# One-hots by pairs of tokens, six landing buffers and whole weight units in a two-layer s5, NSA and PEER kernel

## The chip, the cores and the metric

The kernel runs on 1 core of one Trainium2 chip. The metric is the device time of one execution in microseconds (us). A core has TensorE (PE: matmuls, with its weight loads listed apart as PEld), VectorE (DVE), ScalarE (ACT), GpSimd (POOL), and SyncE (SP), whose DMA queue brings the weights here.

## The reference

Two layers on 256 tokens of width 1024. Layer 0 mixes the tokens with an s5 state-space mixer, layer 1 with NSA attention; after each mixer comes a PEER layer: each token picks 16 of 16384 one-vector experts for each of 8 heads. Most of the time goes into PEER:

```python
def peer(h, w_q, sub_keys, u_tab, v_tab):
    qk = (h @ w_q).reshape(b, s, H, 2, PEER_HALF)
    sc = jnp.einsum('bshcd,hckd->bshck', qk, sub_keys)
    s1, i1 = lax.top_k(sc[..., 0, :], K)
    s2, i2 = lax.top_k(sc[..., 1, :], K)
    cand = (s1[..., :, None] + s2[..., None, :]).reshape(b, s, H, K * K)
    cidx = (i1[..., :, None] * PEER_NKEYS + i2[..., None, :]).reshape(b, s, H, K * K)
    top_s, top_pos = lax.top_k(cand, K)
    experts = jnp.take_along_axis(cidx, top_pos, axis=-1)
    gates = jax.nn.softmax(top_s, axis=-1)
...
        act = jax.nn.gelu(jnp.einsum('cd,ced->ce', hc, u)) * gc    # u = u_tab[experts]
        return jnp.einsum('ce,ced->cd', act, v)                    # v = v_tab[experts]
```

Around both stands `x = x + g * f(modulate(rmsnorm(x), sh, sc))`, with g, sh and sc from one product of the condition vector with `ada_w`; at the end comes an rmsnorm.

## The kernel before

Everything is held transposed (features on the 128 partitions, tokens along the row). The kernel doesn't gather experts: in each PEER layer it multiplies the hidden state with all 16384 rows of `peer_u`, in 128 units of 128x1024 32-bit values (512 KB), applies gelu, multiplies by a dense matrix of gates that is zero wherever no expert was picked, and multiplies the result, B (128 partitions x 128 x 256 tokens), with all 128 units of `peer_v`.

*Weight units.* `load_unit` (L126) brings a unit by SP's queue into one of five `raw` buffers (RAW, L25). `split_w` (L144) makes from it a rounded part w_hi (ACT, L139) and a rest w_lo (DVE, L181), each as two halves of 128x512, in rings of four buffers. `mm3` (L184 to 190) does three matmuls of 256 columns for each 128 rows: w_hi with h_hi, w_hi with h_lo, w_lo with h_hi; a unit has 8 x 3 of them. `chunk_T` does one unit; a `Pair` does two units in turns (at the input projection, glu, the first head of each routing, the first keys and the output projection).

*PEER's stages.* `route_steps` scores the keys and picks the top 16 with DVE's MAX, MAX_INDEX and MATCH_REPLACE (L863 to 867); `decode` turns positions into indices and gates (L919 to 943, with POOL's products at L931) and puts them into `slotT` by a transposition. `G` builds the dense gates for four tokens at a time, in 64 groups a layer: one-hots `oi` and `oj` of the picked row and column (DVE, L760 and 761), `oh` and `ol`, the column's one-hot times the two 16-bit parts of the gate (DVE L762, POOL L763), then eight 16-bit matmuls that sum the outer products into a PSUM bank (L767, L768), and a multiplication into B by DVE (L771) where gelu has been done already, or a copy by ACT (L774) where it hasn't (then L738 multiplies later). `VS` (L790 ff.) does the second product: per unit 12 matmuls of 512 columns into four banks (L797).

*Order.* Each engine takes its instructions in the program's order. That order is set by the tile scheduler by priorities and its own estimate of each operation; splits of weights have a higher priority (PRIO). `weave` puts U (the first product's units) beside the routing and then beside G, by the rough costs that each step yields. In `decode` DVE's order, and in VS DVE's and SP's order, is as written.

## Time and profile before

| | |
|---|---|
| time of 3 runs | median 2117.07 us (2114.87 to 2120.47) |
| profiled execution, its own time | 2114.4 us |
| span in its trace | 2112.6 us, 39866 instructions |
| mean granted clock of TensorE | 0.983 |
| PE busy | 2052.1 us, 97% |
| DVE busy | 1667.1 us, 79% |
| ACT busy | 1163.2 us, 55% |
| POOL busy | 271.0 us, 13% |
| DMA queue of the weights | 371.42 MB, 55.1% of 16 engines' span |

Busy time is the union of an engine's instructions; matmuls overlap in the pipeline, so that the duration of one says less than the distance of two starts. The span is that of the trace; the execution's own time lies around it.

### The profile page before, as it was taken

What the parts mean: (1) busy time and instruction counts of PE and PEld (TensorE: products, weight loads), DVE (VectorE), ACT (ScalarE), POOL (GpSimd) and SP (SyncE); (2) the same over time, 40 slices, a digit from 0 to 9 for tenths busy, and PEclk for the clock granted to TensorE, in tenths of its full rate; (3) what the DMA queues carried; (4) which work ended last, traced back from release to release, by engine and by line L of the source; (5) the groups of instructions that cost most, each with busy time, mean ns of one, the idle gap of its engine ahead of it and who ended that gap; (6) DMA issues with size and microseconds to landing.
All of it is one profiled execution on the core that took longest, in us unless ns stands there. A gap on an engine that the chain in (4) does not pass through costs nothing.

```text
span 2112.6 us, 39866 instructions
## 1 busy us (share of the span) xinstructions
PE 2052.1 (97%) x14344; PEld 1855.0 (88%) x14344; DVE 1667.1 (79%) x3826; ACT 1163.2 (55%) x2392; POOL 271.0 (13%) x277
## 2 busy tenths in 40 slices
PE   6899999999999999999999999999999999999998
PEld 3688999899999988888898689998999998888887
DVE  8696899889898777777766769999988975665655
ACT  4775555555445555555545655555554455555554
POOL 4230002223331000000010000023332300000000
PEclk8899999999999999999999999999999999999999
DMA  7445455544445888878863035554444456666663
GB/s 264 170 161 160 161 179 170 152 145 134 140 137 179 259 274 269 272 270 270 269 215 102 20 121 170 170 170 150 138 140 135 138 172 185 194 197 191 197 191 109
DMA packets 102695, 377.23 MB, mean 179 GB/s; under 512 B 11488, under 2 KB 11872, under 8 KB 101472
## 3 DMA queue, kind: packets, MB, share of 16 engines
q1 hardware_dynamic: 101520, 371.42, 55.1%
q0 software_dynamic: 544, 2.61, 0.4%
q8 instruction: 112, 1.84, 0.4%
q14 instruction: 87, 0.71, 0.1%
q10 hardware_dynamic: 432, 0.65, 0.1%
HBM read 373.07 MB, written 1.05 MB: 177 GB/s over the span
## 4 chain that ended last, share of the span: by engine, by line
PE 90%; DVE 6%; ACT 2%; issue 1%; DMA 0%; POOL 0%; DVEq 0%; ACTq 0%; POOLq 0%
PE bank L797 33%; PE bank L190 15%; PE bank L189 14%; PE bank L188 14%; PE bank L767 3%; PE bank L768 3%; DVE w_lo L181 2%; PE bank L1189 1%; PE bank L874 1%; PE bank L1152 1%; PE bank L1067 1%; PE bank L613 1%; PE bank L1150 1%; PE bank L1177 1%; PE bank L584 1%
## 5 line engine op out<-in xcount | busy, mean ns | idle before, releaser
L139 ACT ACTIVATE w_hi<-raw 128x512 fp32r<-128x512 f32 x1194 | 747.4, 629 | 641.4 <-PE bank L189 336.6
L181 DVE TENSOR_TENSOR w_lo<-raw,w_hi 128x512 fp32r<-128x512 f32 x1194 | 826.3, 715 | 120.4 <-ACT w_hi L139 117.8
L188 PE MATMUL bank<-h_hi,w_hi 128*128 128x256 f32 x2504 | 719.2, 290 | 10.6 <-ACT w_hi L139 7.2
L190 PE MATMUL bank<-h_hi,w_lo 128*128 128x256 f32 x2504 | 711.9, 287 | 13.2 <-DVE w_lo L181 13.0
L189 PE MATMUL bank<-h_lo,w_hi 128*128 128x256 f32 x2504 | 711.9, 285 | 1.0 <-DVE h_lo L304 1.0
L188 PEld LDWEIGHTS bank<-h_hi,w_hi 128*128 128x128 f32 x2504 | 483.5, 194 | 19.0 <-ACT w_hi L139 9.9
L190 PEld LDWEIGHTS bank<-h_hi,w_lo 128*128 128x128 f32 x2504 | 481.1, 193 | 18.0 <-DVE w_lo L181 17.6
L189 PEld LDWEIGHTS bank<-h_lo,w_hi 128*128 128x128 f32 x2504 | 484.2, 193 | 3.3 <-DVE h_lo L304 2.1
L797 PE MATMUL bank<-w_lo,a_hi 128*128 128x512 f32 x1024 | 398.9, 390 | 0.5 <-DVE w_lo L181 0.5
L797 PE MATMUL bank<-w_hi,a_lo 128*128 128x512 f32 x1024 | 398.5, 389 | 0.0
L797 PE MATMUL bank<-w_hi,a_hi 128*128 128x512 f32 x1024 | 281.3, 389 | 0.0
L181 DVE TENSOR_TENSOR a_lo<-B,a_hi 128x256 fp32r<-128x256 f32 x256 | 108.8, 425 | 193.6 <-ACT a_hi L139 193.6
L797 PEld LDWEIGHTS bank<-w_lo,a_hi 128*128 128x128 f32 x1024 | 192.2, 188 | 40.3 <-DVE w_lo L181 1.2
L797 PEld LDWEIGHTS bank<-w_hi,a_lo 128*128 128x128 f32 x1024 | 192.3, 188 | 40.0
L797 PEld LDWEIGHTS bank<-w_hi,a_hi 128*128 128x128 f32 x1024 | 191.4, 188 | 38.6
L763 POOL TENSOR_TENSOR ol<-oj,slotT 128x512 f16<-128x512 f16 x128 | 155.3, 1221 | 335.9 <-PE bank L768 323.8
L774 ACT ACTIVATE B<-bank 128x296 f32<-128x296 f32 (+31 forms) x128 | 67.6, 528 | 148.4 <-DVE B L771 148.4
L768 PE MATMUL bank<-ol,oi 128*128 128x128 f16 x512 | 126.6, 297 | 0.0
L767 PE MATMUL bank<-oh,oi 128*128 128x128 f16 x512 | 125.7, 295 | 0.0
L139 ACT ACTIVATE a_hi<-B 128x256 fp32r<-128x256 f32 x256 | 106.8, 418 | 27.3 <-PE bank L797 14.6
L771 DVE SCALAR_TENSOR_TENSOR B<-bank,B 128x216 f32<-128x216 f32 (+31 forms) x128 | 114.4, 893 | 1.1 <-ACT B L734 0.8
L762 DVE TENSOR_TENSOR oh<-oj,slotT 128x512 f16<-128x512 f16 x128 | 58.6, 459 | 42.7 <-PE bank L767 42.3
(267 smaller groups left out, 2067.8 us busy)
## 6 DMA issues: line engine op xcount, KB each, us to landing
raw<-peer_u SPq DMA_DIRECT2D x256, 512.0 KB, 3.6
raw<-peer_v SPq DMA_DIRECT2D x256, 512.0 KB, 4.3
raw<-ada_t SPq DMA_DIRECT2D x56, 512.0 KB, 4.3
raw<-ada_w SPq DMA_DIRECT2D x40, 512.0 KB, 5.3
raw<-w_q SPq DMA_DIRECT2D x32, 512.0 KB, 3.5
raw<-w_glu SPq DMA_DIRECT2D x16, 512.0 KB, 4.3
raw<-w_in SPq DMA_DIRECT2D x8, 512.0 KB, 4.8
w<-w_cmp SPq DMA_DIRECT2D x4, 1024.0 KB, 9.7
```

Of the source, the lines that this page charges most:

```text
L139: nc.scalar.activation(hi, raw, AF.Copy)
L181: K.nc.vector.tensor_tensor(lo, raw, hi.bitcast(F32), op=OP.subtract)
L188: nc.tensor.matmul(out, wh, xh, start=start, stop=False)
L189: nc.tensor.matmul(out, wh, xl, start=False, stop=False)
L190: nc.tensor.matmul(out, wl, xh, start=False, stop=stop)
L762: V.tensor_tensor(oh, oj, sl[2], op=OP.mult)
L763: nc.gpsimd.tensor_tensor(ol, oj, sl[3], op=OP.mult)
L767: nc.tensor.matmul(pv[:, t], oi[:, :, t], oh[:, :, t], start=True, stop=False)
L768: nc.tensor.matmul(pv[:, t], oi[:, :, t], ol[:, :, t], start=False, stop=True)
L771: V.scalar_tensor_tensor(Bv[:, ts, :jd], pv[:, :, :jd], 1.0 / GS, Bv[:, ts, :jd], op0=OP.mult, op1=OP.mult)
L774: nc.scalar.activation(Bv[:, ts, jd:], pv[:, :, jd:], AF.Copy, scale=1.0 / GS)
L797: nc.tensor.matmul(acc[t][dh], a[al][:, ts], w[wl], start=(j == 0 and al + wl == 0), stop=(j == NJ - 1 and al == 1))
```

## The change

The constant `iota4` (each number four times) becomes `iota2` (twice). G makes all one-hots of a group in one comparison of 1024 values (`oij`: two pairs of tokens, row or column, 128 places, two tokens) and both products with the gate in one multiplication of 1024 (`ohl`), both on DVE; POOL has no part in it. `slotT` gets the matching order, written by two ACT operations where one stood. The matmuls read their operands at a step of two 16-bit values where it was four, and write their result at a step of four 32-bit values where it was without gaps; the multiplication into B then runs over B and the bank in the order in which both lie. A unit's w_hi and w_lo are made by one operation of 128x1024 each, in rings of two buffers. RAW becomes 6, `ge` has one buffer, and `cact` lies in layer 0's pool.

```diff
@@ -22,7 +22,7 @@
 DEPTH = 2
 EPS = 1e-6
 PRIO = 200
-RAW = 5
+RAW = 6
 TWO_PI = 2.0 * math.pi
 C1 = 6.28125
 C2 = TWO_PI - C1
@@ -58,15 +58,10 @@
     nc.scalar.dma_start(K.cst, aps["consts"])
     K.ident = K.cst[:, 0:P]
     K.iota = K.cst[:, P:2 * P]
-    K.iota4 = K.const.tile([P, 4 * P], F16, name="iota4")
-    nc.vector.tensor_copy(K.iota4.rearrange("p (j t) -> p j t", t=4), K.iota[:, :, None].to_broadcast([P, P, 4]))
+    K.iota2 = K.const.tile([P, P, 2], F16, name="iota2")
+    nc.vector.tensor_copy(K.iota2, K.iota[:, :, None].to_broadcast([P, P, 2]))
     K.ones = K.const.tile([P, P], F32, name="ones")
     nc.vector.memset(K.ones, 1.0)
-
-
-    K.cact = K.const.tile([P, KC, 32], F32, name="cact")
-    nc.gpsimd.memset(K.cact, 0.0)
-    silu(K, K.cact[:, :, 0], small(K, "c"))
 
     K.mod = [K.const.tile([P, 48], F32, name=f"mod{i}") for i in range(DEPTH)]
 
@@ -77,6 +72,11 @@
             break
         with tc.tile_pool(name=f"x{layer}", bufs=1, reuse_waits="tile") as xp:
             K.xp = xp
+            if not layer:
+
+                K.cact = xp.tile([P, KC, 32], F32, name="cact")
+                nc.gpsimd.memset(K.cact, 0.0)
+                silu(K, K.cact[:, :, 0], small(K, "c"))
             if layer:
                 peer_end(K, 0, acc)
             mixer(K)
@@ -144,15 +144,14 @@
 def split_w(K, raw):
 
     with K.tc.high_priority(offset=PRIO):
-        return [split(K, raw[:, i * 512:(i + 1) * 512], [P, 512], "w", bufs=4) for i in range(2)]
+        return split(K, raw, [P, 1024], "w", bufs=2)
 
 
 def chunk_T(K, w, x, out):
 
     for k in range(KC):
-        hi, lo = w[k // 4]
-        cs = slice((k % 4) * P, (k % 4 + 1) * P)
-        mm3(K, out, (hi[:, cs], lo[:, cs]), (x[0][:, k], x[1][:, k]), k == 0, k == KC - 1)
+        cs = slice(k * P, (k + 1) * P)
+        mm3(K, out, (w[0][:, cs], w[1][:, cs]), (x[0][:, k], x[1][:, k]), k == 0, k == KC - 1)
 
 
 class Pair:
@@ -164,10 +163,9 @@
         self.ps = [bank(K)[:, :S] for _ in srcs]
 
     def add(self, k):
-        cs = slice((k % 4) * P, (k % 4 + 1) * P)
+        cs = slice(k * P, (k + 1) * P)
         for w, ps in zip(self.ws, self.ps):
-            hi, lo = w[k // 4]
-            mm3(self.K, ps, (hi[:, cs], lo[:, cs]), (self.x[0][:, k], self.x[1][:, k]), k == 0, k == KC - 1)
+            mm3(self.K, ps, (w[0][:, cs], w[1][:, cs]), (self.x[0][:, k], self.x[1][:, k]), k == 0, k == KC - 1)
 
 
 def pair_T(K, srcs, x):
@@ -716,7 +714,7 @@
             tc.tile_pool(name=f"pw{layer}", bufs=2, reuse_waits="tile") as wp, ExitStack() as es:
 
         B = pp.tile([P, NJ, S], F32, name="B")
-        slotT = pp.tile([P, 4, S], F16, name="slotT")
+        slotT = pp.tile([P, 2, S // 2, 2, 2], F16, name="slotT")
         done = [0]
         ugelu = [0]
         u_src, v_src = K.aps["peer_u"], K.aps["peer_v"]
@@ -733,7 +731,7 @@
                 if t0 < S:
                     nc.scalar.activation(out[:, :, t0:], pv[:, :, t0:], AF.Gelu_apprx_tanh)
                 if t0 > 0:
-                    g = wp.tile([P, 2, S], F32, name="ge")
+                    g = wp.tile([P, 2, S], F32, name="ge", bufs=1)
                     nc.scalar.activation(g[:, :, :t0], pv[:, :, :t0], AF.Gelu_apprx_tanh)
                     V.tensor_mul(out[:, :, :t0], g[:, :, :t0], out[:, :, :t0])
                 ugelu[0] = 2 * c + 2
@@ -751,27 +749,29 @@
 
         def G(gp):
 
-            tab = K.iota4.rearrange("p (j t) -> p j t", t=4)
+            tab = K.iota2
+            full = [P, 4, P, 2]
             for q in range(S // 4):
                 ts = slice(4 * q, 4 * q + 4)
-                t4 = lambda name: gp.tile([P, P, 4], F16, name=name)
-                oi, oj, oh, ol = t4("oi"), t4("oj"), t4("oh"), t4("ol")
-                sl = [slotT[:, n, None, ts].to_broadcast([P, P, 4]) for n in range(4)]
-                V.tensor_tensor(oi, tab, sl[0], op=OP.is_equal)
-                V.tensor_tensor(oj, tab, sl[1], op=OP.is_equal)
-                V.tensor_tensor(oh, oj, sl[2], op=OP.mult)
-                nc.gpsimd.tensor_tensor(ol, oj, sl[3], op=OP.mult)
+
+                oij, ohl = (gp.tile([P, 2, 2, P, 2], F16, name=n) for n in ("oij", "ohl"))
+                si, sg = (slotT[:, n, 2 * q:2 * q + 2].rearrange("p a n t -> p (a n) t")[:, :, None, :].to_broadcast(full)
+                          for n in range(2))
+                V.tensor_tensor(oij.rearrange("p a n j t -> p (a n) j t"), tab[:, None].to_broadcast(full), si,
+                                op=OP.is_equal)
+                oj = oij[:, :, 1, None].to_broadcast([P, 2, 2, P, 2])
+                V.tensor_tensor(ohl, oj, slotT[:, 1, 2 * q:2 * q + 2, :, None, :].to_broadcast([P, 2, 2, P, 2]), op=OP.mult)
                 ps = bank(K)
-                pv = ps.rearrange("p (t j) -> p t j", t=4)
+                pv = ps.rearrange("p (j t) -> p j t", t=4)
                 for t in range(4):
-                    nc.tensor.matmul(pv[:, t], oi[:, :, t], oh[:, :, t], start=True, stop=False)
-                    nc.tensor.matmul(pv[:, t], oi[:, :, t], ol[:, :, t], start=False, stop=True)
+                    for n in range(2):
+                        nc.tensor.matmul(pv[:, :, t], oij[:, t // 2, 0, :, t % 2], ohl[:, t // 2, n, :, t % 2],
+                                         start=(n == 0), stop=(n == 1), skip_group_check=True)
                 jd = ugelu[0]
-                Bv = B.rearrange("p j t -> p t j")
-                V.scalar_tensor_tensor(Bv[:, ts, :jd], pv[:, :, :jd], 1.0 / GS, Bv[:, ts, :jd],
+                V.scalar_tensor_tensor(B[:, :jd, ts], pv[:, :jd], 1.0 / GS, B[:, :jd, ts],
                                        op0=OP.mult, op1=OP.mult)
                 if jd < NJ:
-                    nc.scalar.activation(Bv[:, ts, jd:], pv[:, :, jd:], AF.Copy, scale=1.0 / GS)
+                    nc.scalar.activation(B[:, jd:, ts], pv[:, jd:], AF.Copy, scale=1.0 / GS)
                 done[0] = 4 * q + 4
                 yield 0.5, 1.5
 
@@ -790,11 +790,13 @@
                 raw = load_unit(K, v_src[layer, j])
                 with tc.high_priority(offset=PRIO):
                     a = split(K, B[:, j], [P, S], "a", pool=vp)
-                for dh, w in enumerate(split_w(K, raw)):
+                w = split_w(K, raw)
+                for dh in range(2):
+                    ds = slice(dh * 512, dh * 512 + 512)
                     for t in range(2):
                         ts = slice(t * P, (t + 1) * P)
                         for al, wl in ((0, 0), (0, 1), (1, 0)):
-                            nc.tensor.matmul(acc[t][dh], a[al][:, ts], w[wl],
+                            nc.tensor.matmul(acc[t][dh], a[al][:, ts], w[wl][:, ds],
                                              start=(j == 0 and al + wl == 0), stop=(j == NJ - 1 and al == 1))
                 yield j
 
@@ -944,7 +946,10 @@
         ps = bank(K)
         for i, a in enumerate((sel[:, 0], sel[:, 1], e, el)):
             nc.tensor.transpose(ps[:, i * P:(i + 1) * P], a.rearrange("p h k -> p (h k)"), K.ident)
-        nc.scalar.activation(slotT[:, :, t * P:(t + 1) * P], ps.rearrange("p (a t) -> p a t", a=4), AF.Copy)
+
+        pv = ps.rearrange("p (g n a t) -> p g n a t", g=2, n=2, t=2)
+        for g in range(2):
+            nc.scalar.activation(slotT[:, g, t * P // 2:(t + 1) * P // 2].rearrange("p a n t -> p n a t"), pv[:, g], AF.Copy)
         yield 0.4, 0.2
 
     for u in range(9):
@@ -1107,8 +1112,10 @@
 
     pv = [bank(K) for _ in range(2)]
     for k2 in range(KC // 2):
-        for kk, w in enumerate(split_w(K, load_unit(K, aps["w_v"][k2]))):
+        wu = split_w(K, load_unit(K, aps["w_v"][k2]))
+        for kk in range(2):
             k = 2 * k2 + kk
+            w = [x[:, kk * 512:kk * 512 + 512] for x in wu]
             for t in range(2):
                 ts = slice(t * P, (t + 1) * P)
                 nc.tensor.matmul(pv[t], h[0][:, k, ts], w[0], start=(k == 0), stop=False)
```

DVE where one-hots are built beside weight units in layer 0, before: `w_lo` is a half of a weight unit, L738 multiplies gelu values into B, L771 multiplies a bank of gates into B.
```order
L181 TENSOR_TENSOR w_lo<-raw,w_hi 128x512
L761 TENSOR_TENSOR oj<-iota_71,slotT 128x512
L738 TENSOR_TENSOR B<-ge,B 128x2x116
L181 TENSOR_TENSOR w_lo<-raw,w_hi 128x512
L762 TENSOR_TENSOR oh<-oj,slotT 128x512
L771 SCALAR_TENSOR_TENSOR B<-bank,B 128x4x78
L760 TENSOR_TENSOR oi<-iota_71,slotT 128x512
L181 TENSOR_TENSOR w_lo<-raw,w_hi 128x512
L761 TENSOR_TENSOR oj<-iota_71,slotT 128x512
L181 TENSOR_TENSOR w_lo<-raw,w_hi 128x512
L762 TENSOR_TENSOR oh<-oj,slotT 128x512
L771 SCALAR_TENSOR_TENSOR B<-bank,B 128x4x78
```
The same place now, from the same column counts of L771 on.
```order
L179 TENSOR_TENSOR w_lo<-raw,w_hi 128x1024
L763 TENSOR_TENSOR ohl<-oij,slotT 128x1024
L760 TENSOR_TENSOR oij<-iota_71,slotT 128x1024
L179 TENSOR_TENSOR w_lo<-raw,w_hi 128x1024
L771 SCALAR_TENSOR_TENSOR B<-bank,B 128x78x4
L763 TENSOR_TENSOR ohl<-oij,slotT 128x1024
L736 TENSOR_TENSOR B<-ge,B 128x2x116
L771 SCALAR_TENSOR_TENSOR B<-bank,B 128x78x4
L760 TENSOR_TENSOR oij<-iota_71,slotT 128x1024
L179 TENSOR_TENSOR w_lo<-raw,w_hi 128x1024
```
A half's w_lo stood after one to three other operations; a whole unit's w_lo now stands after two to five, and the two operations on one-hots stand where four did (one of them was POOL's).

DVE in the routing of layer 0, before: L863 to L867 are the steps of the top 16 of a head, on scores of 128 or sums of 256.
```order
L865 MATCH_REPLACE B<-B 128x128 x2
L181 TENSOR_TENSOR w_lo<-raw,w_hi 128x512 x2
L866 MAX B<-B 128x8 x2
L181 TENSOR_TENSOR w_lo<-raw,w_hi 128x512
L867 MAX_INDEX B<-B 128x8
L906 TENSOR_TENSOR B<-B 128x256
L867 MAX_INDEX B<-B 128x8
L906 TENSOR_TENSOR B<-B 128x256
L181 TENSOR_TENSOR w_lo<-raw,w_hi 128x512
```
The routing of layer 0 now; the same steps are L865 to L869.
```order
L179 TENSOR_TENSOR w_lo<-raw,w_hi 128x1024
L865 MAX B<-B 128x8 x4
L866 MAX_INDEX B<-B 128x8
L867 MATCH_REPLACE B<-B 128x128
L866 MAX_INDEX B<-B 128x8
L867 MATCH_REPLACE B<-B 128x128
L866 MAX_INDEX B<-B 128x8 x2
L868 MAX B<-B 128x8 x2
L179 TENSOR_TENSOR w_lo<-raw,w_hi 128x1024
```
Before, one to four steps of the top 16 or sums (L906) stand between two halves' w_lo; now up to twelve stand between two w_lo.

PE where the first pair of layer 0's routing ends and the third unit begins, before: bank_2721 is the second result of the pair, bank_2773 that of the third unit; a number stands for one buffer.
```order
L189 MATMUL bank_2720<-h_lo_2663,w_hi_2706 128x256
L190 MATMUL bank_2720<-h_hi_2662,w_lo_2707 128x256
L188 MATMUL bank_2721<-h_hi_2662,w_hi_2716 128x256
L189 MATMUL bank_2721<-h_lo_2663,w_hi_2716 128x256
L190 MATMUL bank_2721<-h_hi_2662,w_lo_2717 128x256
L188 MATMUL bank_2773<-h_hi_2662,w_hi_2776 128x256
L189 MATMUL bank_2773<-h_lo_2663,w_hi_2776 128x256
L190 MATMUL bank_2773<-h_hi_2662,w_lo_2777 128x256
```
The same place now: bank_2616 and bank_2617 are the pair's results, bank_2669 and bank_2701 those of the third and fourth unit, and L876 is the scores' product of a head.
```order
L186 MATMUL bank_2616<-h_hi_2566,w_hi_2606 128x256
L187 MATMUL bank_2616<-h_lo_2567,w_hi_2606 128x256
L188 MATMUL bank_2616<-h_hi_2566,w_lo_2607 128x256
L186 MATMUL bank_2617<-h_hi_2566,w_hi_2612 128x256
L187 MATMUL bank_2617<-h_lo_2567,w_hi_2612 128x256
L188 MATMUL bank_2617<-h_hi_2566,w_lo_2613 128x256
L186 MATMUL bank_2669<-h_hi_2566,w_hi_2672 128x256
L187 MATMUL bank_2669<-h_lo_2567,w_hi_2672 128x256
L186 MATMUL bank_2701<-h_hi_2566,w_hi_2704 128x256
L187 MATMUL bank_2701<-h_lo_2567,w_hi_2704 128x256
L876 MATMUL bank_2603<-B_2600 128x128 x2
L188 MATMUL bank_2669<-h_hi_2566,w_lo_2673 128x256
```
Before, the pair's last matmul is followed by the third unit's in the usual order of three. Now two units' first w_hi matmuls and the scores' product stand ahead of the third unit's first w_lo matmul.

## Rows read from the trace of the kernel before

**Rows 1.** The page: busy time of each engine in the whole execution (busy us, share of the span, instructions), and the chain of work that ended last by engine.
```profile
PE 2052.1 (97%) x14344; PEld 1855.0 (88%) x14344; DVE 1667.1 (79%) x3826; ACT 1163.2 (55%) x2392; POOL 271.0 (13%) x277
PE 90%; DVE 6%; ACT 2%; issue 1%; DMA 0%; POOL 0%; DVEq 0%; ACTq 0%; POOLq 0%
```
**Rows 2.** The table by stretches of time. Columns: the stretch and its length in us, then busy us and number of instructions of PE, PEld, DVE, ACT and POOL, then PE's granted clock, the DMA share and GB/s. The three stretches lie in layer 0's routing, in layer 0's building of one-hots, and in layer 1's second product with B.
```profile
240.00:340.00 100.00, 100.00 (x839) 100.00 (x839) 98.64 (x393) 53.13 (x93) 0.00 (x0) 1.00 0.55 173
500.00:600.00 100.00, 100.00 (x839) 98.58 (x838) 87.30 (x171) 48.37 (x105) 30.20 (x26) 1.00 0.44 138
1900.00:2000.00 100.00, 100.00 (x443) 82.81 (x442) 59.74 (x111) 57.75 (x111) 0.00 (x0) 1.00 0.64 194
```
**Rows 3.** The timeline of PE from 550 to 556 us, where one-hots are multiplied between weight units. Columns here and in the other timelines: start in us, duration in us, engine, line, operation, result and operands, count; in brackets the wait ahead of it and what ended that.
```profile
554.41 0.29 PE L767 MATMUL bank<-oh,oi 128*128 128x128 f16 x1
554.52 0.30 PE L768 MATMUL bank<-ol,oi 128*128 128x128 f16 x1
...
555.23 0.29 PE L768 MATMUL bank<-ol,oi 128*128 128x128 f16 x1
555.27 0.37 PE L188 MATMUL bank<-h_hi,w_hi 128*128 128x256 f32 x1
555.48 0.28 PE L189 MATMUL bank<-h_lo,w_hi 128*128 128x256 f32 x1
```
**Rows 4.** The timeline of PE from 1150 to 1156 us, in the attention of layer 1: 16-bit matmuls of 128 columns without steps.
```profile
1152.92 0.23 PE L1154 MATMUL bank<-maskb,identb 128*128 128x128 bf16 x1
1152.99 0.22 PE L1155 MATMUL bank<-maskb,identb 128*128 128x128 bf16 x1
```
**Rows 5.** The timeline of PE from 136 to 146 us, in the s5 mixer.
```profile
138.17 1.09 PE L618 MATMUL bank<-rH,wo 128*32 128x63 f32 x64
139.07 1.06 PE L512 MATMUL bank<-wo,bpad 128*32 128x128 f32 x32
```
**Rows 6.** The view by lines and shapes, of 70 to 165 us (first row) and of the whole span (second). Columns: line, engine, operation, count, then busy us and mean ns of one, then the idle time ahead.
```profile
L613 PE MATMUL bank<-u,T 128*128 128x64 f32 x16 | 3.4, 300 | 0.0
L1067 PE MATMUL bank<-kp,w 128*128 128x60 f32 x128 | 14.6, 288 | 0.0
```
**Rows 7.** The same view of the whole span, of DVE, ACT and POOL.
```profile
L181 DVE TENSOR_TENSOR w_lo<-raw,w_hi 128x512 fp32r<-128x512 f32 x1194 | 826.3, 715 | 120.4 <-ACT w_hi L139 117.8 <-PE bank L190 0.6 <-PE bank L189 0.5
L139 ACT ACTIVATE w_hi<-raw 128x512 fp32r<-128x512 f32 x1194 | 747.4, 629 | 641.4 <-PE bank L189 336.6 <-issue 199.6 <-PE bank L797 69.2
L763 POOL TENSOR_TENSOR ol<-oj,slotT 128x512 f16<-128x512 f16 x128 | 155.3, 1221 | 335.9 <-PE bank L768 323.8 <-DVE oj L761 6.7 <-ACT w_hi L139 5.4
L139 ACT ACTIVATE a_hi<-B 128x256 fp32r<-128x256 f32 x256 | 106.8, 418 | 27.3 <-PE bank L797 14.6
L233 DVE SCALAR_TENSOR_TENSOR raw<-raw,cb 128x1024 f32<-128x1024 f32 x56 | 68.3, 1219 | 0.0
```
**Rows 8.** The timeline of DVE from 550 to 562 us.
```profile
551.96 0.93 DVE L771 SCALAR_TENSOR_TENSOR B<-bank,B 128x328 f32<-128x328 f32 x1
552.80 0.43 DVE L760 TENSOR_TENSOR oi<-iota,slotT 128x512 f16<-128x512 f16 x1
553.14 0.68 DVE L181 TENSOR_TENSOR w_lo<-raw,w_hi 128x512 fp32r<-128x512 f32 x1
553.75 0.42 DVE L761 TENSOR_TENSOR oj<-iota,slotT 128x512 f16<-128x512 f16 x1
554.08 0.44 DVE L738 TENSOR_TENSOR B<-ge,B 128x280 f32<-128x280 f32 x1
```
**Rows 9.** The timeline of PE and ACT from 550 to 556 us: the last matmul that reads a w_hi tile, and the next w_hi.
```profile
550.35 0.28 PE L189 MATMUL bank<-h_lo,w_hi 128*128 128x256 f32 x1
550.73 0.63 ACT L139 ACTIVATE w_hi<-raw 128x512 fp32r<-128x512 f32 x1 [0.70 <-PE bank L189]
```
**Rows 10.** The waits of PE over the whole span, by what was late: total us, number of waits, longest of them.
```profile
PE bank L190 <- DVE w_lo L181: 13.0, 16, 2.0
```
**Rows 11.** The timeline of DVE from 362 to 412 us, the decoding of layer 0's routing.
```profile
374.92 1.30 DVE L181 TENSOR_TENSOR w_lo<-raw,w_hi 128x512 fp32r<-128x512 f32 x2
376.14 0.28 DVE L936 TENSOR_TENSOR B<-B 128x128 f32<-128x128 f32 x1
378.59 0.29 DVE L938 TENSOR_REDUCE B<-B 128x8 f32<-128x128 f32 x1 [2.17 <-ACT B L937]
...
381.22 0.29 DVE L943 TENSOR_TENSOR B<-B 128x128 f32<-128x128 f32 x1 [1.78 <-ACT B L941]
...
382.23 1.29 DVE L181 TENSOR_TENSOR w_lo<-raw,w_hi 128x512 fp32r<-128x512 f32 x2
```
**Rows 12.** The timelines of POOL and DVE from 333 to 362 us, where the decoding begins.
```profile
349.94 4.52 POOL L931 TENSOR_TENSOR B<-B 128x512 f32<-128x512 f32 x2 [133.33 <-DVE B L929]
351.59 3.42 DVE L181 TENSOR_TENSOR w_lo<-raw,w_hi 128x512 fp32r<-128x512 f32 x2
```
**Rows 13.** The timeline of PE and ACT from 1850 to 1856 us, in the second product with B of layer 1.
```profile
1852.61 1.07 PE L797 MATMUL bank<-w_hi,a_hi 128*128 128x512 f32 x4
1852.97 0.62 ACT L139 ACTIVATE w_hi<-raw 128x512 fp32r<-128x512 f32 x1
...
1855.33 0.84 PE L797 MATMUL bank<-w_hi,a_hi 128*128 128x512 f32 x3
```

## The prediction

> **What bounds the kernel now.** I read the page's busy times first, then the same by stage, then the waits of TensorE, then the timeline of the stage that the change touches. TensorE (PE) is busy 2052.1 of 2112.6 us and carries 90% of the chain that ended last [rows 1]. [...] While the routing runs, VectorE (DVE) is almost as full, 98.64 of 100. While the one-hots are built it has 12.7 us of 100 left over. PE's whole loss to late w_lo tiles is 13.0 us in 16 waits [rows 10]. So a change that relieves DVE or ScalarE (ACT) gives time back only in those 13 us; otherwise it must make PE's own work shorter, or it makes PE wait.
>
> **The change, part by part.**
>
> *The one-hot matmuls.* There are 1024 of them, 8 for each of 128 groups of four tokens. Their number and operand sizes stay; their steps in memory change. Before, both operands are read at a step of four 16-bit values (8 bytes), and the result is written without gaps. From 554.41 to 555.48 us eight of them and one weight matmul of 0.12 us start, so (1.07 - 0.12) / 8 = 0.119 us each [rows 3]. A matmul of the same size without any step, L1154, is followed by the next after 0.07 us [rows 4]; with the two decimals shown, 0.065 fits its neighbours. The step therefore costs about 0.054 us. [...] But the result is now written to every fourth 32-bit value. Only L618 and L613 write like that. The 64 matmuls of L618 take 139.07 - 138.17 = 0.90 us [rows 5], in 16 groups of four that share the array side by side, so 0.056 us for 63 columns or 0.89 ns a column. L613 is slower, but L1067, which reads with a step and writes without gaps, takes 288 ns for 60 columns against L613's 300 ns for 64 [rows 6]: that cost is the reading's, and the step of the result adds nothing to it. No row shows a stepped result written faster than 0.89 ns a column. 128 columns at that rate are 0.114 us, and with a few ns between matmuls 0.119 us is what they cost now. The ends are 0.065 us (-0.054 x 1024 = -55 us) and 0.125 us (+6 us). I take the row that writes as the new code writes, L618: no gain, 0 us.
>
> [...]
>
> *The one-hot operations.* Three DVE operations of 512 16-bit values and one on GpSimd (POOL, 1221 ns [rows 7]) become two on DVE of 1024. The old ones follow one another after 0.34 us (552.80 to 553.14, 553.75 to 554.08 [rows 8]). With the fixed part of about 0.07 us that the f32 operation shows (0.61 us for 512 values, 553.14 to 553.75) the new ones cost 0.07 + 2 x 0.27 = 0.61 us each if they keep the 16-bit rate, 1.13 us if they fall to the f32 rate. The two together are 1.22 us against 1.02 before; the multiplication into B (0.93 us for 328 values [rows 8], because it walks through B at a large step) becomes contiguous and should fall to about 0.45 us. DVE needs less, not more, and PE is the bound of the stage: 0 us. If the rate is lost, see the rivals.
>
> *Whole units.* Two w_lo operations of 0.61 us become one of about 1.15 us (the same engine does 1024 values with an accumulation in 1219 ns), two w_hi of 629 ns become one of 629 + (629 - 418) x 2 = 1.05 us [rows 7]. Both engines save a little; what counts is when. ACT starts w_hi 0.38 us after the start of the last matmul that reads the buffer (550.35 to 550.73 [rows 9]). Before, four half buffers stood in a ring: a half freed was wanted again 3 x 1.43 us later and ready after 0.38 + 0.63 + 0.68 us, so about 2.5 us to spare. Now the last w_hi matmul of a unit is its 23rd; from the unit's start, w_hi of the unit after next begins at 22 x 0.119 + 0.38 = 3.0 us, ends at 4.05 and w_lo ends at 5.3 us. It is wanted at 2 x 2.86 + 0.24 = 5.96 us. Some 0.6 us are left where 2.5 were. Three places use that up.
>
> Routing: 839 matmuls are 35 units, so DVE spends 98.64 / 35 = 2.8 us a unit, 1.2 of it on w_lo and 1.6 on sorting [rows 2]. A head's 32 sorting operations spread over five units, 6.4 a unit, 0.25 us each; the new order (the fences on the routing, under the change) puts runs of 12 between two w_lo, 3.0 us. From one w_lo to the next that is 4.15 us against a period of 2.9; 0.6 us of the 1.25 are covered, 0.65 lost, once in each of 16 heads: +10 us (0 to +22).
>
> Pairs: after a pair of units that are read in turns both buffers come free only at its end. From the last matmul that reads the first w_hi, the next w_lo is there after 0.38 + 1.05 + 1.15 + 0.1 = 2.7 us; PE has some 1.1 us of matmuls to do (the fences on the pair). That is 1.6 us, at five places (glu, both routings, the first keys, the output projection): +8 us (+4 to +10).
>
> Decoding the routing: DVE makes no w_lo from 376.14 to 382.23 us, since L938 and L943 wait for ACT [rows 11], and in front of that POOL's first product (4.52 us) holds up DVE's w_lo for 3.42 us [rows 12]. The old ring covered part of each; the lost cover of 2 us costs up to +4 us a layer. Against it stands that POOL's one-hot product is gone, which shares this stretch: -1.5 us a layer. Together +5 us (-4 to +14).
>
> The second product with B takes 1855.33 - 1852.61 = 2.72 us a unit [rows 13]. There the four w_hi matmuls stand first, w_lo is wanted only 0.9 us into the unit, and ACT and DVE have a third of their time free: 0 us, up to +5. The sixth landing buffer adds nothing: no wait of PE in the trace is for a transfer. The moved cact and the single ge buffer: 0, +-3 us.
>
> The sum: 0 + 10 + 8 + 5 = +23 us on the profiled execution's 2114.4 us, 2137.4. The median of the runs shown, 2117.07, lies 2.7 us above that execution, so I forecast a median of 2140 us.
>
> **The rivals.**
>
> B, faster: the stepped result costs nothing. Then 1024 matmuls drop to 0.065 us, -55 us, and the other terms stay: 2117 - 55 + 23 = 2085 us. For it: the 4-byte read step is certain to be no worse, and L618 could be held by its own 32-bit rate and not by the write. It decides if the new matmul starts follow closer than 0.1 us. DVE would then need about 2 x 0.61 + 1.15 + 0.45 + 0.25 = 3.1 us for a group and a unit against PE's 3.4: still covered.
>
> C, no change: the result is as slow as the old reads, and DVE, relieved in each unit, catches up, so that the tighter ring costs only a few us: 2117 to 2124, say 2120 us. Against it: 98.64 of 100 leaves little to catch up with.
>
> D, much slower: pairs of two 16-bit values lose DVE's 16-bit rate. A group and a unit then cost DVE 2 x 1.13 + 1.15 + 0.45 + 0.25 = 4.1 us against PE's 3.82; 0.3 us x 128 = +38 us, 2178 us. Against it: the old operations keep the rate with runs of four.
>
> **How the numbers follow.** Forecast A 0.52 (its own range 2124 to 2160), B 0.29 (2070 to 2100), C 0.14, D 0.05. No more than 2 in 10 may lie outside, so the range must reach into B: 2078 to 2160. About 0.3% is what a measurement of this kernel can tell from no change, 6.4 us. Faster: B and a little of C, 0.31. Within: most of C and the low end of A, 0.15. Slower: 0.54.
>
> **What would show it.** Starts of the new one-hot matmuls 0.119 us apart show the first step right, 0.065 show B. PE's waits for w_lo, 13.0 us now, should rise to 30 to 40 us, in routing and decoding, with waits of 1 to 2 us right after each pair. DVE's two one-hot operations should last near 0.7 us; 1.2 us means D. The forecast is wrong above all if the one-hot matmuls get faster, or if the waits for w_lo do not grow.

## The result and the profile after

The changed kernel takes 2131.84 us in the median of 4 runs (2127.32 to 2133.93), the kernel before 2115.97 us on the same chip (4 runs, 2114.86 to 2120.47): a ratio of 1.0068, 95% interval 1.0046 to 1.009, by which it is some 14 us slower (the medians lie 16 us apart). The profiled execution is the fastest of the four: 2127.32 us, with a span of 2125.5 us, 12.9 us more than before.

The page's busy times of the changed kernel, which answer to [rows 1]:

```profile
PE 2052.3 (97%) x14344; PEld 1846.7 (87%) x14344; DVE 1578.2 (74%) x3101; ACT 1035.0 (49%) x1799; POOL 119.1 (6%) x149
```

DVE works 89 us less, ACT 128, POOL 152, and the time grows: none of the three set the pace. PE is busy as long as before, which hides that it gained in one stage and lost in others. The table by stretches shows it (columns as in [rows 2]):

```profile
240.00:340.00 100.00, 97.40 (x803) 96.04 (x802) 97.39 (x366) 44.37 (x61) 0.00 (x0) 1.00 0.53 165
500.00:600.00 100.00, 100.00 (x852) 98.29 (x851) 79.90 (x121) 42.06 (x79) 0.00 (x0) 1.00 0.45 140
1900.00:2000.00 100.00, 100.00 (x443) 82.79 (x442) 60.92 (x74) 50.01 (x75) 0.00 (x0) 1.00 0.64 194
```

In the routing PE gets through 803 matmuls in 100 us where it did 839; while one-hots are built, 852 where it did 839; in the second product 443 as before. Idle time shows only 2.6 (100 - 97.40) of the 4.3 us that the 36 missing matmuls of the routing are worth (36 x 0.119): one matmul's record lasts 0.28 us and the next starts after 0.12, so that a wait under some 0.16 us doesn't show as idle.

To see where the time went I compared the starts of matmuls that occur in one place, by the view of one source line. Of layer 0, L876 and L768 after, L874 and L767 before (columns: minimum, median and maximum of the duration in ns, then first and last start):

```profile
L876 PE MATMUL bank<-B x64: 271/275/276, 225.1 to 334.1; 128*128 128x128 f32 x64
L768 PE MATMUL bank<-ohl,oij x512: 272/310/311, 423.8 to 664.5; 128*128 128x128 f16 x171
```
```profile
L874 PE MATMUL bank<-B x64: 272/275/347, 221.3 to 323.4; 128*128 128x128 f32 x64
L767 PE MATMUL bank<-oh,oi x256: 277/296/299, 412.1 to 659.3; 128*128 128x128 f16 x128
```

From the first to the last score the changed kernel takes 109.0 us and the kernel before 102.1. But by the program's order 22 more weight matmuls stand in that stretch now, 22 x 0.119 = 2.6 us of work that another stretch no longer has; the loss is 4.3 us. Done so for every stretch, both layers added:

| stretch (us against before) | forecast | changed | e1 | e9 | e11 | e7 | e3 | e12 |
|---|---|---|---|---|---|---|---|---|
| start to first scores (glu, one pair of routing) | pairs | +6.4 | -1.2 | +1.7 | +1.5 | +38.2 | +7.8 | -0.4 |
| routing, 2 layers | +10 | +8.7 | -0.2 | +4.8 | +7.8 | +0.1 | +10.3 | 0.0 |
| decoding to first one-hots, 2 layers | +5 | -3.2 | -3.8 | -3.9 | -1.8 | -12.3 | -3.1 | -10.2 |
| one-hots with the units beside them, 2 layers | 0 | -8.0 | -9.0 | -9.2 | -8.1 | 0.0 | -45.8 | -56.1 |
| second product, 2 layers | 0 | +0.8 | -0.4 | 0.0 | +0.8 | +9.1 | +1.2 | -0.5 |
| end of layer 0 to layer 1's scores (three pairs) | pairs | +8.7 | -4.1 | +6.9 | +6.3 | +12.3 | +10.0 | -2.1 |
| rest | 0 | -0.5 | -0.3 | +0.5 | -0.3 | +0.2 | -0.3 | -0.2 |
| span | +23 | +12.9 | -19.0 | +0.8 | +6.2 | +47.6 | -19.9 | -69.5 |

(e1 and the others are the experiments below. Pairs were forecast at +8 in the two stretches together. The stretch into layer 1's scores is uncertain by some 5 us: three kernels with halves, alike in it, gave -4.1, +6.7 and -1.3 there (e1, e5, e6). Most of the scatter is layer 1's attention, which no edit touches: 88.4 us before at a granted clock of 0.98, 89.0 in the changed kernel at 1.00, 86.8 in e1 at 1.00, 92.0 in e11 at 0.96, 96.1 in e5 at 0.89.)

The one-hot stage in the changed kernel, PE's timeline and then DVE's:

```profile
551.11 1.05 PE L768 MATMUL bank<-ohl,oij 128*128 128x128 f16 x8
551.91 0.36 PE L188 MATMUL bank<-h_hi,w_lo 128*128 128x256 f32 x1
552.12 0.28 PE L186 MATMUL bank<-h_hi,w_hi 128*128 128x256 f32 x1
```
```profile
552.20 0.69 DVE L760 TENSOR_TENSOR oij<-iota,slotT 128x1024 f16<-128x1024 f16 x1 [0.93 <-PE bank L768]
552.81 1.22 DVE L179 TENSOR_TENSOR w_lo<-raw,w_hi 128x1024 fp32r<-128x1024 f32 x1
553.94 0.49 DVE L771 SCALAR_TENSOR_TENSOR B<-bank,B 128x328 f32<-128x328 f32 x1
554.35 0.68 DVE L763 TENSOR_TENSOR ohl<-oij,slotT 128x1024 f16<-128x1024 f16 x1
554.95 0.42 DVE L736 TENSOR_TENSOR B<-ge,B 128x264 f32<-128x264 f32 x1
```

Eight one-hot matmuls and one of weights take 552.12 - 551.11 = 1.01 us, so (1.01 - 0.12) / 8 = 0.111 us each, against 0.119 in [rows 3]. DVE follows on after 0.61 us (one-hots), 1.13 (w_lo) and 0.41 (into B): it kept the 16-bit rate (0.61 us for 1024 values; the f32 w_lo takes 1.13 for as many).

PE's waits (total us, times, longest), to set beside [rows 10]:

```profile
PE bank L186 <- ACT w_hi L139: 15.6, 17, 4.2
PE bank L188 <- DVE w_lo L179: 14.3, 13, 2.3
```

The waits for w_hi before, which the rows ahead don't show:

```profile
PE bank L188 <- ACT w_hi L139: 7.2, 2, 3.8
```

In layer 0's routing PE waits five times, all in its first half, three times for w_lo and twice for w_hi (from the timeline of PE; layer 1's has the same five):

```profile
241.49 0.39 PE L188 MATMUL bank<-h_hi,w_lo 128*128 128x256 f32 x1 [0.35 <-DVE w_lo L179]
...
254.97 0.39 PE L188 MATMUL bank<-h_hi,w_lo 128*128 128x256 f32 x1 [0.68 <-DVE w_lo L179]
...
261.77 0.38 PE L186 MATMUL bank<-h_hi,w_hi 128*128 128x256 f32 x1 [0.34 <-ACT w_hi L139]
...
272.10 0.39 PE L186 MATMUL bank<-h_hi,w_hi 128*128 128x256 f32 x1 [0.79 <-ACT w_hi L139]
...
275.66 0.39 PE L188 MATMUL bank<-h_hi,w_lo 128*128 128x256 f32 x1 [0.43 <-DVE w_lo L179]
```

The largest new waits stand where glu's first two units end. PE, and below it ACT:

```profile
161.51 0.28 PE L188 MATMUL bank<-yh,w_lo 128*128 128x256 f32 x1
162.59 0.38 PE L186 MATMUL bank<-yh,w_hi 128*128 128x256 f32 x1 [0.80 <-ACT w_hi L139]
162.81 0.28 PE L187 MATMUL bank<-yl,w_hi 128*128 128x256 f32 x1
165.23 0.38 PE L186 MATMUL bank<-yh,w_hi 128*128 128x256 f32 x1 [2.14 <-ACT w_hi L139]
...
165.74 0.42 PE L186 MATMUL bank<-yh,w_hi 128*128 128x256 f32 x1
165.96 0.42 PE L187 MATMUL bank<-yl,w_hi 128*128 128x256 f32 x1
...
168.73 0.41 PE L188 MATMUL bank<-yh,w_lo 128*128 128x256 f32 x1
168.94 0.32 PE L186 MATMUL bank<-yh,w_hi 128*128 128x256 f32 x1
169.10 0.28 PE L187 MATMUL bank<-yl,w_hi 128*128 128x256 f32 x1
```
```profile
161.48 1.06 ACT L139 ACTIVATE w_hi<-raw 128x1024 fp32r<-128x1024 f32 x1 [1.46 <-PE bank L187]
162.55 1.28 ACT L652 ACT_TABLE_LOAD   x1
163.84 0.38 ACT L652 ACTIVATE sg<-bank 128x256 f32<-128x256 f32 x1
164.12 1.05 ACT L139 ACTIVATE w_hi<-raw 128x1024 fp32r<-128x1024 f32 x1
```

Both w_hi buffers come free only as the pair ends. ACT then splits one unit, loads a table, does a sigmoid and only then splits the second. After these waits PE's matmuls start 0.21 us apart for 3.2 us, from 168.94 on 0.12. The granted clock of that stretch (the last but two of the columns) is 0.50:

```profile
165.70:168.90 3.20, 3.20 (x17) 3.20 (x16) 1.49 (x3) 0.42 (x1) 0.00 (x0) 0.50 0.72 232
```

The other four pairs show two waits for w_hi each as well, 1.13 to 1.51 us a pair. With glu's 2.94 these ten waits come to 8.4 us of idle time.

### The profile page after: what moved, and what is told of

The parts are those of the page before. It is cut to its first block, busy times and chain, and to the rows that moved or that the text cites. A ratio compares the mean times of both kernels' runs of the same rounds, so it can differ in the third digit from the quotient of the medians.

```text
span 2125.5 us, 37126 instructions
## 1 busy us (share of the span) xinstructions
PE 2052.3 (97%) x14344; PEld 1846.7 (87%) x14344; DVE 1578.2 (74%) x3101; ACT 1035.0 (49%) x1799; POOL 119.1 (6%) x149
## 5 line engine op out<-in xcount | busy, mean ns | idle before, releaser
L179 DVE TENSOR_TENSOR w_lo<-raw,w_hi 128x1024 fp32r<-128x1024 f32 x597 | 746.2, 1250 | 251.1 <-ACT w_hi L139 249.6
L139 ACT ACTIVATE w_hi<-raw 128x1024 fp32r<-128x1024 f32 x597 | 628.2, 1053 | 520.7 <-PE bank L187 475.4
L188 PE MATMUL bank<-h_hi,w_lo 128*128 128x256 f32 x2504 | 727.2, 291 | 14.4 <-DVE w_lo L179 14.3
L186 PE MATMUL bank<-h_hi,w_hi 128*128 128x256 f32 x2504 | 719.0, 289 | 16.1 <-ACT w_hi L139 11.5
L186 PEld LDWEIGHTS bank<-h_hi,w_hi 128*128 128x128 f32 x2504 | 483.7, 194 | 26.2 <-ACT w_hi L139 14.8
L799 PE MATMUL bank<-w_hi,a_hi 128*128 128x512 f32 x1024 | 274.4, 390 | 0.0
L768 PE MATMUL bank<-ohl,oij 128*128 128x128 f16 x1024 | 144.5, 305 | 0.0
L760 DVE TENSOR_TENSOR oij<-iota,slotT 128x1024 f16<-128x1024 f16 x128 | 89.8, 703 | 51.8 <-PE bank L768 51.8
L768 PEld LDWEIGHTS <-oij 128*128 128x128 f16 x1024 | 97.8, 123 | 8.0
L771 DVE SCALAR_TENSOR_TENSOR B<-bank,B 128x216 f32<-128x216 f32 (+31 forms) x128 | 62.4, 487 | 51.5 <-PE bank L768 51.5
L774 ACT ACTIVATE B<-bank 128x296 f32<-128x296 f32 (+31 forms) x128 | 42.1, 329 | 96.5 <-DVE B L771 96.5
L763 DVE TENSOR_TENSOR ohl<-oij,slotT 128x1024 f16<-128x1024 f16 x128 | 87.3, 683 | 0.0
```

The costliest lines, as they stand in the source:

```text
L139: nc.scalar.activation(hi, raw, AF.Copy)
L179: K.nc.vector.tensor_tensor(lo, raw, hi.bitcast(F32), op=OP.subtract)
L186: nc.tensor.matmul(out, wh, xh, start=start, stop=False)
L188: nc.tensor.matmul(out, wl, xh, start=False, stop=stop)
L760: V.tensor_tensor(oij.rearrange("p a n j t -> p (a n) j t"), tab[:, None].to_broadcast(full), si, op=OP.is_equal)
L763: V.tensor_tensor(ohl, oj, slotT[:, 1, 2 * q:2 * q + 2, :, None, :].to_broadcast([P, 2, 2, P, 2]), op=OP.mult)
```

## The experiments

All ratios are to the kernel before, run on the same chip. Of longer edits the main lines are shown; `...` stands for lines left out.

**e1, halves.** The changed kernel with the split as before:

```diff
-        return split(K, raw, [P, 1024], "w", bufs=2)
+        return [split(K, raw[:, i * 512:(i + 1) * 512], [P, 512], "w", bufs=4) for i in range(2)]
...
```


> The changed kernel with its weight units split in halves again (four buffers of 128x512 each for hi and lo); one-hots, RAW 6 and the rest stay. First theory: the two halves of the change pull against each other; the new one-hots give back about 4 us a layer (their matmuls follow at 0.111 us, not 0.118) and 1.6 us a layer in the decoding, the whole units cost about 21 us. Then this kernel is faster than before: 2105 to 2112 us, PE's waits for w_hi go back from 15.6 to about 7 us. Rival: the loss comes from the new one-hot operations in DVE's queue (or from RAW 6, ge or cact), not from the units: then 2125 to 2133 us, as the changed kernel.

Measured: 2095.99 us, 0.9927 [0.9909, 0.9946], faster than either theory had it. The whole units cost 1.0068 - 0.9927 = 1.4%, some 30 us, and everything else in the change gives 15 us. The table puts the 30 us at the pairs and in the routing. No stretch of e1 loses time, so RAW, `ge` and `cact` show no cost.

**e2, units.** The changed kernel with G, `slotT` and the table of before:

```diff
...
-                V.tensor_tensor(ohl, oj, slotT[:, 1, 2 * q:2 * q + 2, :, None, :].to_broadcast([P, 2, 2, P, 2]), op=OP.mult)
...
+                V.tensor_tensor(oi, tab, sl[0], op=OP.is_equal)
+                V.tensor_tensor(oj, tab, sl[1], op=OP.is_equal)
+                V.tensor_tensor(oh, oj, sl[2], op=OP.mult)
+                nc.gpsimd.tensor_tensor(ol, oj, sl[3], op=OP.mult)
...
```

> The changed kernel with the one-hots of before (four operations a group, one of them on POOL, operands at a step of 8 bytes, results without gaps); units split whole, two buffers, RAW 6 stay. First theory: the units alone cost 21 us and the one-hots' gain of 8 to 11 us is missing: 2137 to 2145 us; one-hot matmuls at 0.118 us. Rival (the one-hots cost the time): 2112 to 2120 us, as before. Second rival (each part does little, they collide in DVE's queue): both this and the kernel with halves lie within 4 us of before.

Measured: 2153.4 us, 1.0203 [1.0179, 1.0228], above every expected range: the units are the loss, and more of one than the first theory had. Its profiled execution, the fastest of four (span 2144.0 us), lost 31.4 us; what the other three (up to 2157.94 us) lost on top no trace shows.

**e3, results without gaps.** The changed kernel with

```diff
-                pv = ps.rearrange("p (j t) -> p j t", t=4)
+                pv = ps.rearrange("p (t j) -> p t j", t=4)
...
-                        nc.tensor.matmul(pv[:, :, t], oij[:, t // 2, 0, :, t % 2], ohl[:, t // 2, n, :, t % 2],
+                        nc.tensor.matmul(pv[:, t], oij[:, t // 2, 0, :, t % 2], ohl[:, t // 2, n, :, t % 2],
```

and B read and written at a step again, as in G before.

> The changed kernel with the results of the one-hot matmuls written without gaps (token after token) and read by DVE and ACT at a step, as before; operands stay at a step of 4 bytes. Theory of the prediction: the stepped result is what holds the matmuls at 0.111 us; then they fall to about 0.065 us, 0.046 x 1024 = 47 us less: 2080 to 2092 us, unless DVE's multiplication into B (0.93 us again) makes PE wait. Rival: the reading of the one-hots (as weights or moving) at any step is the limit; then 0.10 to 0.119 us and 2126 to 2140 us.

Measured: 2092.04 us, 0.9903 [0.9879, 0.9927], at the upper end of the theory's range. PE's timeline:

```profile
563.70 0.63 PE L768 MATMUL bank<-ohl,oij 128*128 128x128 f16 x8
564.14 0.36 PE L188 MATMUL bank<-h_hi,w_lo 128*128 128x256 f32 x1
564.34 0.28 PE L186 MATMUL bank<-h_hi,w_hi 128*128 128x256 f32 x1
```

(0.64 - 0.12) / 8 = 0.065 us each, where the stepped result took 0.111. For the matmuls nothing but the order in the bank differs, so the stepped result costs 0.046 us a matmul, 47 us in all. Of these 38 arrive in the stage (-45.8 against -8.0): DVE, which again needs 0.9 us for the multiplication into B, is busy 98.23 of 100 us there. Where it has room again, in e6 and e12 below, all 47 arrive (-56.1 against -9.0 in e1).

```profile
500.00:600.00 100.00, 100.00 (x933) 98.00 (x932) 98.23 (x131) 51.03 (x88) 0.00 (x0) 1.00 0.49 150
```

**e4, operands without a step too.** e3 with the one-hots laid out token by token:

```diff
...
-                        nc.tensor.matmul(pv[:, t], oij[:, t // 2, 0, :, t % 2], ohl[:, t // 2, n, :, t % 2],
+                        nc.tensor.matmul(pv[:, t], oij[:, t // 2, 0, t % 2], ohl[:, t // 2, n, t % 2],
```

> As the kernel with results without gaps, and with the one-hots laid out token by token, so that the matmuls read both operands without any step (the two gate products become two operations, and DVE's one-hot operations repeat one value along the row, so they may be slow). It shows the floor: both theories expect starts 0.06 to 0.07 us apart. If the kernel with a step of 4 bytes reads as fast as this one, the operands' step is free; if these are faster still, the step of 4 bytes costs the difference. DVE's one-hot operations of 1024: 0.7 us if they keep the 16-bit rate, 1.2 us if they lose it; then the time of the whole kernel says nothing on the matmuls.

Measured: 2211.49 us, one run. The group of eight lasts as long as in e3 (0.62 us against 0.63), so the operands' step of 4 bytes is free. DVE lost its 16-bit rate. A group on PE, and the comparison on DVE:

```profile
563.24 0.62 PE L769 MATMUL bank<-ohl,oij 128*128 128x128 f16 x8
```
```profile
L760 DVE TENSOR_TENSOR oij<-iota,slotT 128x1024 f16<-128x1024 f16 x128 | 157.4, 1231 | 2.9 <-PE bank L769 2.9
```

1231 ns where the pairs of tokens need 703: that is what rival D feared of the pairs, and what came where one operand repeats a value along the row.

**e5 and e6, halves and results without gaps.** e6 walks B in its own order besides:

```diff
-                V.scalar_tensor_tensor(Bv[:, ts, :jd], pv[:, :, :jd], 1.0 / GS, Bv[:, ts, :jd],
+                pj = ps.rearrange("p (t j) -> p j t", t=4)
+                V.scalar_tensor_tensor(B[:, :jd, ts], pj[:, :jd], 1.0 / GS, B[:, :jd, ts],
...
```


> Weight units in halves and results of the one-hot matmuls without gaps, both at once; the rest as in the changed kernel. If the two are independent (units about 1.4% with the new one-hots, the stepped result about 1.9%), the time is 1.0 - 0.0073 - 0.019 = 0.974 of before, 2050 to 2062 us. Rival: DVE, which is busy 98 of 100 us in the one-hot stage of the kernel with flat results alone, becomes the bound there (halves cost it 0.2 us more a unit): then 2064 to 2080 us, with PE's waits for w_lo above 20 us.

> As the kernel with halves and results without gaps, but DVE and ACT walk through B in its own order (four tokens side by side) and through the bank at a step of 512 bytes. If the large step through B is what makes the multiplication take 0.9 us for 328 values and the bank's step is free, it falls to about 0.49 us, as in the changed kernel, DVE has some 15 us of 100 left in the one-hot stage, and the time is 2046 to 2056 us. Rival: a step through the bank costs DVE the same as one through B: 0.9 us again, and the time of the kernel with halves and results without gaps within 4 us.

Measured: e5 2064.77 us, 0.9763 [0.9734, 0.9792]; e6 2051.32 us, 0.9724 [0.9689, 0.976], as expected. The multiplication into B, e5 and then e6 (the mean of one in ns is the last number before the second bar):

```profile
L774 DVE SCALAR_TENSOR_TENSOR B<-bank,B 128x216 f32<-128x216 f32 (+31 forms) x128 | 115.1, 899 | 9.6 <-PE bank L770 8.4 <-ACT B L734 0.8
```
```profile
L774 DVE SCALAR_TENSOR_TENSOR B<-bank,B 128x216 f32<-128x216 f32 (+31 forms) x128 | 62.6, 489 | 32.9 <-PE bank L770 31.2 <-ACT B L734 0.8
```

DVE in e5 from 500 to 600 us (its busy time is the third of the engines'):

```profile
500.00:600.00 100.00, 98.59 (x930) 97.25 (x929) 99.74 (x158) 52.72 (x115) 0.00 (x0) 1.00 0.48 151
```

e5's time lies between its two theories: just above the range of the first, on the lower edge of the rival's. DVE is full there (99.74 of 100 us), but PE waits for it only in the last 14 of a layer's 64 groups, for `ohl` (7.8 us in 12 waits) and not for w_lo (10.7 us, where the rival had over 20); the stage takes 10 us more than in e6. In e6 the multiplication takes 489 ns against 899 in e5, as little as in the changed kernel (487), so DVE pays for the step through B and not for one through the bank.

**e7, three buffers.**

```diff
-RAW = 6
+RAW = 4
...
-        return split(K, raw, [P, 1024], "w", bufs=2)
+        return split(K, raw, [P, 1024], "w", bufs=3)
```

> The changed kernel (whole units, stepped results) with three buffers each for w_hi and w_lo and, to have the room, four landing buffers. If the loss of the whole units is the shallow ring (two buffers: 0.6 us to spare a unit), one more unit of cover takes nearly all of it back: 2093 to 2103 us, PE's waits for w_hi and w_lo from 29.9 to about 15 us. Rival: the loss is that a split of a whole unit takes 1.05 + 1.25 us before its first use, twice as long as a half, whatever the depth: then 2118 to 2132 us. If four landing buffers are too few, waits for DMA show it.

Measured: 2157.41 us, 1.0205 [1.0165, 1.0245]. Neither theory's time: 38 us went before the first scores, where PE waits 25.2 us for w_hi in six waits, and 9 in the second product, where ACT now waits for transfers:

```profile
ACT w_hi L139 <- DMA raw<-peer_v: 117.0, 90, 4.7
```

That the four landing buffers did both is the likeliest reading, but no run has them alone. In the routing, though, the loss is gone (+0.1 us instead of +8.7): there it was the ring's depth.

**e8, units in turn.** In `pair_T`:

```diff
-    p = Pair(K, srcs, x)
-    for k in range(KC):
-        p.add(k)
+    for src in srcs:
+        ps = bank(K)[:, :S]
+        chunk_T(K, split_w(K, load_unit(K, src)), x, ps)
```

> The changed kernel with the pairs of glu, routing, first keys and output projection computed one unit after the other instead of in turns. If the pairs cost what the trace says (about 17 us between start and routing of both layers, both buffers free only at a pair's end), the time falls by 8 to 17 us, to 2115 to 2124 us, less what the pairs gave where the hidden state arrives piece by piece (not known, 0 to 5 us). Rival: the pairs are not the cause, each first unit waits for its split anyway: 2128 to 2140 us.

Measured: 2129.66 us, 1.0073 [1.0056, 1.009], unchanged. That is the rival's time, but it speaks for neither side: in its trace PE still does the two units of glu side by side, and the waits of 0.80 and 2.13 us are there. The scheduler had put them so.

**e9, half operations in whole buffers.** In `split_w`, `hi` and `lo` being 128x1024 with two buffers:

```diff
...
+        for i in range(2):
+            c = slice(i * 512, i * 512 + 512)
+            K.nc.scalar.activation(hi[:, c], raw[:, c], AF.Copy)
+            sub_lo(K, lo[:, c], raw[:, c], hi[:, c])
```

> The changed kernel, each unit still in one buffer for w_hi and one for w_lo (two of each), but each filled by two operations of 128x512, as before the change. It parts the length of the operations from the size of the buffers. If the size of the buffers costs the time (both free only when the last matmul of a unit, or of a pair, has read them), it stays at 2122 to 2134 us, and PE's waits for w_hi after the pairs stay near 15 us, a little shorter each since 0.63 us of w_hi are enough to start. Rival: the length of the operations costs it (sorting waits behind 1.25 us, a unit starts only after 1.05 + 1.25 us): then routing is as fast as before again and the time falls by 9 us or more, to 2096 to 2118 us.

Measured: 2117.38 us, 1.0025 [1.0004, 1.0045]. The time is the upper end of the rival's range, but the routing is not as fast as before, as the rival had it: its loss only shrinks, to 4.8 us. So both are part of it. The length of the operations costs 1.0068 - 1.0025 = 0.4%, the size of the buffers 1.0025 - 0.9927 = 1.0%, each uncertain by some 0.3%. The waits in glu shrink to 0.37 and 0.33 us:

```profile
162.58 0.39 PE L192 MATMUL bank<-yh,w_hi 128*128 128x256 f32 x1 [0.37 <-ACT w_hi L151]
...
165.31 0.38 PE L192 MATMUL bank<-yh,w_hi 128*128 128x256 f32 x1 [0.33 <-ACT w_hi L151]
```

**e10, three w_hi buffers.** `lo` keeps two:

```diff
-RAW = 6
+RAW = 5
...
+        hi = K.st.tile([P, 1024], F32R, name="w_hi", bufs=3)
...
```

> The changed kernel with three buffers for w_hi, two for w_lo and five landing buffers (for the room). If w_hi's ring sets the loss in the routing and after the pairs, ACT splits a unit ahead while w_lo still waits for its buffer: routing about 2 us a layer better than in the changed kernel, waits for w_hi well under 10 us, in all 2112 to 2124 us. Rival: w_lo's ring sets it (it is freed last, at a unit's end): within 4 us of the changed kernel, 2128 to 2136 us, with PE's waits moved from w_hi to w_lo.

Measured: 2125.14 us, 1.0055 [1.0036, 1.0075], between the two ranges; the waits for w_hi are 11.1 us. The routing's loss falls from 8.7 to 2.1 us, so w_hi's ring is most of it. Some is given back: 5.5 us in the second product, where ACT with five landing buffers waits 22.7 us for transfers in layer 0, and the gain of the one-hots (-0.6 us in that stage instead of -8.0). This goes, in e7 as here, in one place of each layer, where PE waits for `ohl` (2.4 us here, 3.2 in e7).

**e11, units in turn with PE's order fixed.** As e8, and ahead of the loop:

```diff
+    with K.tc.manual_schedule(engines={mybir.EngineType.PE}):
```

> The changed kernel with the pairs of glu, routing, first keys and output projection computed one unit after the other, and PE's order there fixed as written (in the kernel with units in turn the scheduler had put the two units back side by side). If the loss of the pairs is that both buffers come free only at the end, the waits for w_hi of 0.8 and 2.1 us after glu's first two units and of 0.7 us twice after each other pair vanish or halve, and the time falls by 4 to 12 us against the changed kernel, to 2120 to 2128 us, if the later arrival of the hidden state's last pieces does not cost as much. Rival: the waits stay, since ACT is late for another reason (the table load of 1.28 us and the sigmoid stand ahead of the second w_hi): 2129 to 2138 us.

Measured: 2118.61 us, 1.0022 [1.0, 1.0043], by the ratios 10 us less than the changed kernel, as the first theory had it. Its trace is 6.7 us shorter, with 3 us more in layer 1's attention. The waits for w_hi at all five pairs are gone, though ACT still does the table load between two splits. What e8 couldn't show, this does: it is the turns that keep both buffers to the end.

**e12, five halves.** e6 with

```diff
-RAW = 6
+RAW = 5
...
-        return [split(K, raw[:, i * 512:(i + 1) * 512], [P, 512], "w", bufs=4) for i in range(2)]
+        return [split(K, raw[:, i * 512:(i + 1) * 512], [P, 512], "w", bufs=5) for i in range(2)]
```

> The kernel with halves, results without gaps and B walked in its own order, with the room of the sixth landing buffer given to a fifth half buffer each for w_hi and w_lo (RAW 5 again). If the sixth landing buffer does nothing and the depth of the ring is what PE's 10.7 us of waits for w_lo in the decoding hang on, the time falls by 2 to 8 us, to 2043 to 2053 us, and those waits to under 7 us. Rival: landing buffers are what the start and the second product of layer 0 need (with four of them these lost 38 and 9 us): then 2053 to 2070 us, with more waits for DMA.

Measured: 2047.29 us, 0.9704 [0.9666, 0.9741], 3.0% below the kernel before and the fastest of all. PE's waits for w_lo fell from 10.7 to 7.2 us (under 7 were expected) and the decoding gained 6.4 us in the trace. The waits in e6 and then in e12:

```profile
PE bank L190 <- DVE w_lo L181: 10.7, 15, 1.4
```
```profile
PE bank L190 <- DVE w_lo L181: 7.2, 14, 1.5
```

Between the medians of e6 and e12 4 us are less than their intervals can tell apart.

## Why the prediction was right, and where its terms were off

It said 2140 us, and slower; 2131.84 came, inside the likeliest case's own range (2124 to 2160). Step by step:

- *One-hot matmuls, 0 us: the mechanism right, the size 8 us too high.* The row that writes as the new code does, L618, decided rightly between 0.119 and 0.065 us; e3 shows both halves of the argument, 0.065 us once the step in the result is gone. That the operands' step of 4 bytes is no worse than the old one, for which the prediction gives no row, e4 shows: 0.63 us for eight matmuls with it, 0.62 without any. The working had 0.114 us at L618's rate and rounded up to 0.119 for "a few ns between matmuls". Measured were 0.111; 0.008 x 1024 = 8 us, which is the -8.0 of the table. Rival B, which needed matmul starts under 0.1 us, fell with the 0.111.
- *One-hot operations, 0 us: right.* DVE has 20 us of 100 to spare where it had 13, and PE gains nothing by it. Operations follow after 0.61 us as forecast, 0.41 for the multiplication (forecast 0.45). The fixed part in the working, 0.07 us, shows once two lengths are there: 2 x 0.34 - 0.61 = 0.07 us for the one-hots, 2 x 0.61 - 1.13 = 0.09 for w_lo. Rival D fell.
- *Routing, +10 us: the cause and the sum right, the working not.* 8.7 were measured, and e7 and e10 confirm the depth of the ring as the cause; the length of the operations has its part, since half operations in the same ring (e9) leave 4.8. But the working had 0.65 us lost once in each of 16 heads. The trace has ten waits, five a layer, of 0.34 to 0.79 us, all in the first half of the routing, and four of the ten are for w_hi. Ten losses in place of 16, each of some 0.9 us with what idle time hides, make nearly the same sum; that is luck.
- *Pairs, +8 us: that both buffers come free only at a pair's end was right, the wait and the size were off.* The two stretches lost 15 us together. The working counted one late w_lo of 1.6 us a pair. The trace shows two late w_hi (8.4 us idle at the five pairs, and more that idle time doesn't show), since ACT splits the two units in series, at glu with a table load of 1.28 us and a sigmoid between them, and then 3.2 us at a granted clock of 0.50, which no term held. e11 gets back 10 us; what the rest hangs on is open.
- *Decoding, +5 us: wrong in sign.* -3.2 measured. The lost cover, priced at up to 4 us a layer, costs next to nothing (-3.2 against -3.8 in e1 with the old ring). The other half of the term, -1.5 us a layer for POOL's product, for which the prediction gives no row, came near: -1.9 us a layer in e1. No run parts POOL's share of it from that of DVE's two new operations.
- *Second product, landing buffer, cact and ge, 0 us: right.* The second product lost 0.8 us.

So the sum was 10 us too high in the trace: 8 each at the one-hots and in the decoding and 1 in the routing, against which the pairs lost 7 more than forecast. That it came so close is in part luck: errors of 8, 8 and 7 us partly cancel. Rival C (DVE catches up) failed, since routing and pairs did lose: together 24 us. As to what would show it, PE's waits for w_lo were to rise to 30 to 40 us; they stayed at 14.3, and it is w_hi's waits that doubled, from 7.2 to 15.6 us, so 29.9 us in all. The prediction had named waits for w_lo that don't grow as a sign of being wrong, and on this point it was. At the pairs PE asks for w_hi first (L186 in the lines on glu), and the late buffers showed there.

## What to carry to other kernels

A layout change moves a step from one side of an operation to another; price each side by a row of its own, and try the layout that has the step where it is free (here on DVE's reading of the bank: 489 ns with the step, 487 without; e6 against e1, 2% of the time). Halving the number of operations on engines that don't set the pace gained nothing here (e9, with the half operations, is 0.4% faster), and the same bytes in half as many buffers hid less (1.0%, e9 against e1): what counted was when the next buffer was wanted, above all where units are read in turns (e11 gets 10 us back there).
